# A depthwise convolution moved from VectorE to TensorE, in a two-block transformer kernel

## Chip, cores and metric

The kernel runs on one core of one Trainium2 chip. The metric is the device time of one execution in microseconds, the median of several runs. Below, PE is TensorE, PEld its loading of weights, DVE is VectorE, ACT ScalarE, POOL GpSimd; SP is the engine that only issues DMAs.

## What is computed

The reference has two blocks on 256 positions of 1024 channels. The first has two layers with modulation: the vectors `c` and `c_ctx` go through SiLU and a 1024 x 6144 matrix per layer, and give six rows (shift, scale and gate, twice). Layer 0 works on two streams, `x` and `ctx` (512 columns together), layer 1 on `x` alone (256 columns). A layer normalises, modulates, multiplies by `w_in`, and splits the product among four mixers: attention, a Fourier mixer, a convolution module and a pooling mixer. Their results are joined, multiplied by `w_out`, and a gated FFN follows. The second block has dilated attention, a spatial gating unit and another gated FFN, and is not touched by the change. The convolution module, cut to what matters:

```python
def conv_module(a, dw_w, dw_b, ln_g, ln_b, w_pw):
    glu = a[..., :W_CONV] * jax.nn.sigmoid(a[..., W_CONV:])
    y = lax.conv_general_dilated(glu, dw_w[:, None, :], window_strides=(1,), padding=[(15, 15)],
                                 feature_group_count=W_CONV) + dw_b     # 31 taps, each channel by itself
    y = jax.nn.silu(layer_norm(y, ln_g, ln_b))
    return y @ w_pw                                                     # W_CONV = 256
```

## The kernel before

Channels lie on the 128 partitions, positions along the columns; 256 channels are two halves, `f` = 0 and 1. The large products take f32 weights apart into a high part (cast on ACT, L244) and a low one (subtraction on DVE, L246) and do three passes (L274 to L276, or L299 to L301). Weights come in pieces of 512 KB on SP's queue, in the order of use, into four buffers `raw`.

**The start.** SP loads the first quarter of modulation weights for layer 0 (`mod_load`, four pieces), the input `XC` (four pieces), two pieces of `w_in`, the second quarter of the modulation (four) and the third group (four, two pieces of `w_in`, four). TensorE is ordered by hand here: `mod_mm` multiplies the weights with SiLU of `c` in column groups of 32 (tile `p_mod`, L464), `mod_cols` transposes the result into columns; `p_ss` (L531) sums squares over the partitions, `p_rb` (L538) spreads the inverse root, and `in0_k` makes the normalised input (n on ACT, L505 and L506, low part on DVE, L507) and starts the product `p_c` of the convolution's 512 input rows, which is the first main product. The other ten rows of modulation are not done by TensorE: `mod_bg` loads 512 KB per step into one of four buffers `wm` on ACT's queue, behind a one-element copy on POOL (L422) that holds the load back until an earlier operation is done, and DVE does two weighted sums per step (`jg`, L427, and `wm`, L429: called a pair below).

**The order.** Outside the start a planner writes the program: each chain of work is a generator that yields the time it thinks it needs; `spawn` starts one, `tick` moves the clock as TensorE's main products are emitted and lets due chains emit their next step, `join` waits for a chain. SP's queue is in the order of the code. Each engine then works its list in order.

**The convolution.** The gated unit (`sg` on ACT, then L688 on DVE) writes `GP`, with 15 columns of zeros on either side. `conv_diag` makes eight diagonal 128 x 128 matrices per half of the taps' weights (on POOL for layer 0, on ACT for layer 1); they lie in two of the four `wm` buffers. `conv_pe` does eight taps per half on TensorE (`p_cv`, L624), each a product of a diagonal matrix with `GP` shifted by a column; `conv_taps` does the other 23 on DVE, one operation each (L632, L636), and adds TensorE's part (L640). Then `conv_ln` takes the mean and the variance over channels on TensorE (`p_mean`, `p_var`), and normalises. `mod_bg` is spawned with the two tap chains as its conditions, so that in layer 0 the modulation's pairs start when the taps are done.

**After it** come attention (`p_qt` transposes queries and keys, `p_s` scores, `pe` exponentials on ACT with a minimum `ast` from DVE, L740, `pT` copies of the transposed ones, `p_o`), the Fourier mixer (`p_fa`, `p_fy`, `p_fw`), the pooling mixer (`UP`, POOL's sums, `p_pl`), and the output product `p_wo`.

Of the kernel before, what the change touches and what calls it, by code (L numbers as in the profile page):

```python
# [24 lines left out]
F32 = mybir.dt.float32  # L25
# [3 lines left out]
OP = mybir.AluOpType  # L29
AX = mybir.AxisListType  # L30

D = 1024
# [6 lines left out]
GW = T + 2 * PAD  # L39
# [6 lines left out]
NPE = 8  # L46
CVD, FOD = 0.9, 1
BG0, BG1 = 2.4, 2.0
SPL, SPH = {"wo1": 3}, (1,)
# [56 lines left out]
for _n, _w in (("c", 16), ("bmod0", 48), ("bmod1", 48), ("g1_0", 8), ("g1_1", 8), ("g2_0", 8),  # L106
               ("g2_1", 8), ("dw_0", 62), ("dw_1", 62), ("db_0", 2), ("db_1", 2), ("lg_0", 2), ("lg_1", 2),
               ("lb_0", 2), ("lb_1", 2), ("ps_0", 2), ("ps_1", 2), ("n1", 8), ("n2", 8), ("fg", 8), ("bs", 8)):
    PK[_n] = _o
    _o += _w  # L110
# [42 lines left out]
def tile_kernel(ctx, tc, xin, pk_d, rows_d, lc_d, bc_d, wmod0, wmod, win, wout, wfi, wfo, wsm, win2w, win2, wproj, wout2,  # L153
# [30 lines left out]
    V.memset(ones, 1.0)  # L184
    mhalf = cpool.tile([128, 12], F32, name="mhalf")
# [9 lines left out]
    G.tensor_scalar(P("dw_0", 0, 124), P("dw_0", 0, 124), 0.5, None, op0=OP.mult)  # L195
# [40 lines left out]
    def split_to(i):  # L236
        while ld["split"] < min(i, len(halves)):
# [7 lines left out]
            every = SPL.get(halves[j][2], 0) or (1 if j in SPH else 0)  # L245
# [224 lines left out]
    def mod_cols(g):  # L470
# [4 lines left out]
        pt = psm("p_modt")  # L475
# [38 lines left out]
    mod_load(0, 0, 4)  # L514
    for i in range(4):
        SP.dma_start(XC[:, 2 * i:2 * i + 2], xin[:, 2 * i:2 * i + 2])
    dma_to(2)
    mod_load(1, 0, 4)
    mod_load(2, 0, 4)
    dma_to(WB)  # L520
    mod_load(2, 4, 8)
    with tc.manual_schedule(engines={mybir.EngineType.PE}):
        mod_mm(0, 0, 4)
        mod_cols(0)
        new_ss(True)
# [3 lines left out]
        for i in range(4):  # L529
            for n, ss in enumerate(ss_t["ss"]):  # L530
                PE.matmul(p[:, i:i + 1], ss[:, 128 * i:128 * i + 128], ones, start=n == 0, stop=n == 1)  # L531
        r = rsqrt(p[:, :4], 4, 1.0 / D, True)
        ld["lim"] = WB
        split_to(2)
        mod_mm(1, 0, 2)
# [3 lines left out]
        mod_mm(1, 2, 4)  # L539
# [3 lines left out]
        split_to(WB)  # L543
        in0_k(2)
        mod_mm(2, 4, 8)
        in0_k(3, lambda: mod_cols(2))
        for k in range(4, KT):
            in0_k(k)
    ld["lim"] = 10 ** 6
    dma_to(WB + RAW)  # L550
    SP.dma_start(rows, bass.AP(tensor=rows_d.tensor, offset=rows_d.offset, ap=[[0, 128], [1, 512]]))
    SP.dma_start(lc, lc_d)

    SP.dma_start(scb.rearrange("p s n -> p (s n)"), bass.AP(tensor=rows_d.tensor, offset=rows_d.offset + 1536,
                                                            ap=[[0, 128], [1, 2048]]))
    for s in range(2):
        S.activation(scb[:, s], scb[:, s], AF.Silu)
# [5 lines left out]
    for l in range(2):  # L563
# [4 lines left out]
        with ExitStack() as mctx:  # L568
# [6 lines left out]
            UP = mp.tile([128, ns, UW], F32, name="UP")  # L575
            S2 = mp.tile([128, ns, UW], F32, name="S2")
            S4 = mp.tile([128, ns, UW], F32, name="S4")
            G.memset(UP[:, :, 0:POOL_PAD], 0.0)
            G.memset(UP[:, :, POOL_PAD + T:], 0.0)
            U = mp.tile([128, 2, N], F32, name="U")  # L580
# [4 lines left out]
            QT = [mp.tile([128, 2, 256], F32, name=f"QT{s}") for s in streams]  # L585

# [20 lines left out]
            cps = {}  # L607

            def conv_diag(f):

                w = lpool.tile([128, D], F32, tag="wm", name="cdg", bufs=WMB)
                for j in range(NPE):
                    tap = pk[:, PK[f"dw_{l}"] + f * TAPS + j:PK[f"dw_{l}"] + f * TAPS + j + 1]
                    if l == 0:
                        G.tensor_scalar(w[:, 128 * j:128 * j + 128], ident, tap, None, op0=OP.mult)
                    else:
                        S.activation(w[:, 128 * j:128 * j + 128], ident, AF.Copy, scale=tap)
                return w

            def conv_pe(f, w):  # L620

                cps[f] = psm("p_cv")
                for j in range(NPE):
                    PE.matmul(cps[f][:, :N].rearrange("p (s t) -> p s t", t=T), w[:, 128 * j:128 * j + 128],  # L624
                              GP[:, f, :, j:j + T], start=j == 0, stop=j == NPE - 1)
                    tick(0.0017 * N)

            def conv_taps(f, delay):
                y = Y[:, f].rearrange("p (s t) -> p s t", t=T)
                dw = PK[f"dw_{l}"] + f * TAPS  # L630
                per = 0.35 * ns
                V.tensor_scalar(y, GP[:, f, :, NPE:NPE + T], pk[:, dw + NPE:dw + NPE + 1], P(f"db_{l}", f), op0=OP.mult,  # L632
                                op1=OP.add)
                yield per + delay
                for j in range(NPE + 1, TAPS):
                    V.scalar_tensor_tensor(y, GP[:, f, :, j:j + T], pk[:, dw + j:dw + j + 1], y, op0=OP.mult, op1=OP.add)  # L636
                    yield per + delay
                while f not in cps:
                    yield 0.3
                V.tensor_tensor(Y[:, f], cps[f][:, :N], Y[:, f], op=OP.add)  # L640
                yield per
                G.tensor_copy(snap, Y[:, f, 0:1])
                pace[0] = snap
# [3 lines left out]
            def conv_ln(t0, t1):  # L647

                yield from wait(t0, t1)
# [86 lines left out]
            def att_unit(s, t, i, j, pT, sums, sp):  # L736
# [5 lines left out]
                pe = mp.tile([128, 512], F32, tag="pe", name="pe", bufs=PEB)  # L742
# [808 lines left out]
```

## Time and profile before

| | us |
|---|---|
| median of 3 runs (lowest, highest) | 1340.57 (1340.22, 1340.75) |
| the profiled execution | 1341.05 |
| its span in the trace | 1339.3 |
| TensorE busy | 1300.0 (97%) |
| DVE busy | 931.9 (70%) |
| ACT busy | 621.4 (46%) |
| POOL busy | 256.7 (19%) |

The time of a run is taken on the device around the program; the span is from the first to the last instruction in the trace of one more execution. The busy time of TensorE is that of its matmuls, whose loads of weights overlap with it. A share over the whole span says little about one stage; the rows further below are therefore taken by stretches of the span.

### The profile page before, as it was taken

The page shows a single profiled execution, that of the slowest core. Times are in us where ns is not written, and L with a number is a line of the kernel's source. Part 1 is how long each engine was busy: PE and PEld are TensorE (multiplying, and loading weights), DVE is VectorE, ACT ScalarE, POOL GpSimd, SP SyncE. Part 2 cuts the span into 40 slices and gives each one's busy share as a digit, 9 for nine tenths or more (in the row PEclk, how much of TensorE's full clock was granted, in tenths as well). Part 3 has the DMA queues.
Part 4 walks back from the last instruction along what each step waited for, and adds up shares of the span by engine and source line. Part 5 has one row for each costly group of instructions (what it writes and reads, how often), then busy time and mean ns, then how long its engine had stood idle before and what let it go on. Part 6 is the DMA issues. An engine that isn't in the chain of part 4 may idle for free.

```text
span 1339.3 us, 20667 instructions
## 1 busy us (share of the span) xinstructions
PE 1300.0 (97%) x7764; PEld 1107.6 (83%) x7764; DVE 931.9 (70%) x1658; ACT 621.4 (46%) x1045; POOL 256.7 (19%) x310
## 2 busy tenths in 40 slices
PE   5999989899999999999999999999999999999997
PEld 4786569788888888899789999888788889888886
DVE  3697997999883333359667666657675777888754
ACT  4434534322132222245565554445675655655542
POOL 4134543243310000133420000010110002211100
PEclk9999999999999999999999999999999999999999
DMA  9624453677883222334135554675344344555463
GB/s 370 221 79 149 134 173 99 244 250 245 300 299 119 95 86 65 102 130 145 45 106 191 178 187 152 189 259 185 129 147 157 135 160 171 191 190 186 154 190 102
DMA packets 66612, 224.67 MB, mean 168 GB/s; under 512 B 7504, under 2 KB 8656, under 8 KB 66384
## 3 DMA queue, kind: packets, MB, share of 16 engines
q1 hardware_dynamic: 53968, 179.21, 39.8%
q10 hardware_dynamic: 12080, 42.50, 9.5%
q0 software_dynamic: 464, 1.64, 0.3%
q8 instruction: 61, 1.00, 0.3%
q14 instruction: 39, 0.32, 0.1%
HBM read 222.27 MB, written 1.05 MB: 167 GB/s over the span
## 4 chain that ended last, share of the span: by engine, by line
PE 87%; DVE 5%; DMA 2%; ACT 2%; issue 2%; POOL 1%; POOLq 0%; SPq 0%; DVEq 0%; ACTq 0%
PE p_dn L283 6%; PE p_ua L275 5%; PE p_ua L276 5%; PE p_ua L274 4%; PE p_ug L276 4%; PE p_ug L275 4%; PE p_ug L274 4%; PE p_ga L283 3%; PE p_gg L283 3%; PE p_dn L274 3%; PE p_dn L275 3%; PE p_dn L284 3%; PE p_dn L276 3%; PE p_gt L283 2%; PE p_wo L276 2%; PE p_wo L275 2%
## 5 line engine op out<-in xcount | busy, mean ns | idle before, releaser
L246 DVE TENSOR_TENSOR wl<-raw,wh 128x1024 fp32r<-128x1024 f32 (+2 forms) x340 | 393.6, 1159 | 249.2 <-ACT wh L244 247.7
L244 ACT CAST wh<-raw 128x1024 fp32r<-128x1024 f32 (+1 forms) x344 | 333.8, 974 | 317.9 <-PE p_ug L275 86.6
L339 POOL TENSOR_TENSOR ss<-ss,sq 128x256 f32<-128x256 f32 (+1 forms) x43 | 45.3, 1054 | 441.5 <-ACT sq L338 295.1
L275 PE MATMUL p_ua<-A,wh 128*128 128x258 f32 (+2 forms) x368 | 122.3, 332 | 3.5 <-DVE A L365 3.5
L283 PE MATMUL p_dn<-H,wh 128*128 128x512 f32 x352 | 124.1, 397 | 0.0
L276 PE MATMUL p_ug<-A,wl 128*128 128x258 f32 (+2 forms) x368 | 122.3, 332 | 0.0
L276 PE MATMUL p_ua<-A,wl 128*128 128x258 f32 (+2 forms) x368 | 122.1, 332 | 0.0
L275 PE MATMUL p_ug<-A,wh 128*128 128x258 f32 (+2 forms) x368 | 121.9, 331 | 0.0
L274 PE MATMUL p_ua<-A,wh 128*128 128x258 f32 (+2 forms) x368 | 121.6, 331 | 0.0
L274 PE MATMUL p_ug<-A,wh 128*128 128x258 f32 (+2 forms) x368 | 121.6, 331 | 0.0
L429 DVE SCALAR_TENSOR_TENSOR wm<-wm,scb 128x1024 f32<-128x1024 f32 x80 | 98.2, 1232 | 10.8 <-DMA wm<-in_wmod 10.7
L284 PE MATMUL p_dn<-H,wl 128*128 128x256 f32 x352 | 98.5, 281 | 0.0
L283 PEld LDWEIGHTS p_dn<-H,wh 128*128 128x128 f32 x352 | 66.0, 188 | 16.1
L275 PEld LDWEIGHTS p_ua<-A,wh 128*128 128x128 f32 x368 | 69.4, 189 | 11.0 <-DVE A L365 3.9
L275 PEld LDWEIGHTS p_ug<-A,wh 128*128 128x128 f32 x368 | 69.5, 189 | 7.2
L276 PEld LDWEIGHTS p_ua<-A,wl 128*128 128x128 f32 x368 | 69.5, 189 | 6.9
L274 PEld LDWEIGHTS p_ug<-A,wh 128*128 128x128 f32 x368 | 69.3, 188 | 7.0
L274 PEld LDWEIGHTS p_ua<-A,wh 128*128 128x128 f32 x368 | 69.3, 188 | 7.0
L276 PEld LDWEIGHTS p_ug<-A,wl 128*128 128x128 f32 x368 | 69.4, 189 | 6.9
L274 PE MATMUL p_dn<-H,wh 128*128 128x512 f32 (+1 forms) x198 | 72.4, 367 | 0.0
L275 PE MATMUL p_dn<-H,wh 128*128 128x512 f32 (+1 forms) x198 | 72.4, 366 | 0.0
L276 PE MATMUL p_dn<-H,wl 128*128 128x512 f32 (+1 forms) x198 | 72.4, 366 | 0.0
(380 smaller groups left out, 3130.4 us busy)
## 6 DMA issues: line engine op xcount, KB each, us to landing
raw<-in_wfi SPq DMA_DIRECT2D x88, 512.0 KB, 3.8
wm<-in_wmod ACTq DMA_DIRECT2D x80, 512.0 KB, 4.5
raw<-in_win SPq DMA_DIRECT2D x44, 512.0 KB, 3.8
raw<-in_wgu SPq DMA_DIRECT2D x44, 512.0 KB, 3.7
raw<-in_win2w SPq DMA_DIRECT2D x40, 512.0 KB, 4.0
raw<-in_wout SPq DMA_DIRECT2D x24, 512.0 KB, 3.7
raw<-in_wfo SPq DMA_DIRECT2D x32, 384.0 KB, 3.1
raw<-in_wfo SPq DMA_DIRECT2D x32, 320.0 KB, 3.2
```

The costliest lines, as they stand in the source:

```text
L244: S.copy(h[:, :n], raw[:, :n])
L246: (G if every and j % every == 0 else V).tensor_tensor(lo[:, :n], raw[:, :n], h[:, :n].bitcast(F32), op=OP.subtract)
L274: PE.matmul(ps, w[0], a[:, 0], start=first, stop=False, **kw)
L275: PE.matmul(ps, w[0], a[:, 1], start=False, stop=False, **kw)
L276: ins = PE.matmul(ps, w[1], a[:, 0], start=False, stop=last, **kw)
L283: PE.matmul(p.rearrange("p (h n) -> p h n", h=2), w[0], a, start=first, stop=False)
L284: PE.matmul(p[:, 0:256], w[1], a[:, 0], start=False, stop=last)
L339: (eng or G).tensor_tensor(ss[0][:, cs], ss[0][:, cs], sq[:, :n], op=OP.add)
L429: V.scalar_tensor_tensor(w, w, 1.0, scb[:, 0], op0=OP.mult, op1=OP.mult, accum_out=modv[:, l, part, 0, k:k + 1])
```

## The change

**The convolution.** DVE's taps and the diagonal matrices go. `conv_shift` copies the gated rows within the chip's memory: for each half, for each group `g` of 32 channels and each shift `j` of 0 to 3, one DMA on SP's queue takes 32 partitions of `GP` from column `j` on and puts them on partitions 32 j to 32 j + 31 of `GS`; 32 copies per layer. A matmul on such a group then contracts 32 channels times four taps: its weights are 128 x 32, four small diagonal matrices under each other, its output is 32 partitions wide. `conv` does eight steps (of 4 taps, 32 in all, the last one zero) for four groups, 64 matmuls per layer, and ACT adds the bias as it takes the sum (L633). The weights of a half are made by one POOL operation. `conv` is spawned with a delay of 8.0 of the planner's time, and joined before attention starts; the pool that holds `GS` is closed then, and the tiles of the pooling mixer and of attention (`UP`, `S2`, `S4`, `U`, `pe`, `pT`) are opened in its place.

**The modulation.** `mod_bg` has no condition any more; its pacing copy reads the gated rows until the convolution is done.

**The start.** SP loads the input first, then two pieces of modulation weights, one of `w_in`, two, one, the four of the second quarter, all eight of the third group, and then `w_in`. TensorE sums the squares first, in one sum per column instead of two; the modulation products follow. Transposed rows go to the second half of the modulation's own PSUM tile. The low part of the second piece of `w_in` is made by DVE, not POOL. `rows`, `lc`, `scb` are loaded, and the normalised input released for the later products, a little earlier. The SiLU of `scb` (SiLU of `c`'s rows) is written behind the gated unit.

```diff
-NPE = 8
-CVD, FOD = 0.9, 1
+CVS = 8.0
+FOD = 1
...
+    id32 = cpool.tile([128, 32], F32, name="id32")
+    V.tensor_reduce(id32, ident.rearrange("p (g c) -> p c g", c=32), axis=AX.X, op=OP.add)
...
-    mod_load(0, 0, 4)
     for i in range(4):
         SP.dma_start(XC[:, 2 * i:2 * i + 2], xin[:, 2 * i:2 * i + 2])
+    mod_load(0, 0, 2)
+    dma_to(1)
+    mod_load(0, 2, 4)
     dma_to(2)
     mod_load(1, 0, 4)
-    mod_load(2, 0, 4)
+    mod_load(2, 0, 8)
     dma_to(WB)
-    mod_load(2, 4, 8)
...
-        mod_mm(0, 0, 4)
-        mod_cols(0)
-        new_ss(True)
+        new_ss(False)
...
-        split_to(2)
-        mod_mm(1, 0, 2)
+        split_to(1)
+        mod_mm(0, 0, 3)
         rb = psm("p_rb")
...
-        mod_mm(1, 2, 4)
+        mod_mm(0, 3, 4)
+        mod_cols(0)
+        mod_mm(1, 0, 4)
         in0_k(0, lambda: mod_cols(1))
...
             def conv_diag(f):
...
+                w = lpool.tile([128, D], F32, tag="wm", name="cdg", bufs=WMB).rearrange("p (q c) -> p q c", c=32)
+                G.tensor_tensor(w, id32[:, None, :].to_broadcast([128, 32, 32]),
+                                P(f"dw_{l}", 32 * f, 32)[:, :, None].to_broadcast([128, 32, 32]), op=OP.mult)
                 return w
...
+            def conv_shift(f):
+
+                gs = gp.tile([128, 4, ns, SW], F32, tag="GS", name="GS", bufs=2)
+                for g in range(4):
+                    for j in range(4):
+                        SP.dma_start(gs[32 * j:32 * j + 32, g], GP[32 * g:32 * g + 32, f, :, j:j + SW])
+                return gs
+
+            def conv(gss):
+
+                for f in range(2):
+                    p = psm("p_cv")
+                    for j in range(8):
+                        for g in range(4):
+                            PE.matmul(p[32 * g:32 * g + 32, :N].rearrange("p (s t) -> p s t", t=T), cdg[f][:, 4 * j + g],
+                                      gss[f][:, g, :, 4 * j:4 * j + T], start=j == 0, stop=j == 7)
+                        yield 0.35 * ns
+                    yield 0.4
+                    S.activation(Y[:, f], p[:, :N], AF.Identity, bias=P(f"db_{l}", f))
+                    yield 0.6
+                G.tensor_copy(snap, Y[:, 1, 0:1])
                 pace[0] = snap
...
-            cv0 = spawn(conv_taps(0, CVD))
-            cv1 = spawn(conv_taps(1, CVD), 0.5)
-            cv = spawn(conv_ln(cv0, cv1))
+            cvm = spawn(conv([conv_shift(f) for f in range(2)]), CVS)
+            cv = spawn(conv_ln(cvm))
             if l == 0:
+                pace[0] = GP[:, 1, 0, PAD:PAD + 1]
                 spawn(mod_bg([(0, 2, True, BG0), (0, 4, True, BG0), (0, 3, True, BG0), (0, 5, True, BG1),
                               (1, 1, True, BG1), (1, 0, True, BG1), (1, 2, False, BG1), (1, 4, False, BG1),
-                              (1, 3, False, BG1), (1, 5, False, BG1)], cv0, cv1))
+                              (1, 3, False, BG1), (1, 5, False, BG1)]))
...
-            for f in range(2):
-                conv_pe(f, cdg[f])
+
+            join(cvm)
+            gctx.close()
+            ap = mctx.enter_context(tc.tile_pool(name=f"a{l}", bufs=1))
```

The order of instructions shows what the lines make of it. First TensorE's list at the start, before:

```order
L464 MATMUL p_mod<-rawm,scf 32x128 x32
L477 MATMUL p_modt<-ident,row 128x128
L531 MATMUL p_ss<-ones,ss 128x1
L531 MATMUL p_ss<-ones,ssl 128x1
L531 MATMUL p_ss<-ones,ss 128x1
L531 MATMUL p_ss<-ones,ssl 128x1
L531 MATMUL p_ss<-ones,ss 128x1
L531 MATMUL p_ss<-ones,ssl 128x1
L531 MATMUL p_ss<-ones,ss 128x1
L531 MATMUL p_ss<-ones,ssl 128x1
L464 MATMUL p_mod<-rawm,scf 32x128 x16
L538 MATMUL p_rb<-ident,rs_r 128x128 x4
L464 MATMUL p_mod<-rawm,scf 32x128 x16
L274 MATMUL p_c<-A_73,wh 128x512
```
and after:

```order
L532 MATMUL p_ss<-ones,ss 128x1 x4
L467 MATMUL p_mod<-rawm,scf 32x128 x24
L539 MATMUL p_rb<-ident,rs_r 128x128 x4
L467 MATMUL p_mod<-rawm,scf 32x128 x8
L480 MATMUL p_mod<-ident,row 128x128
L467 MATMUL p_mod<-rawm,scf 32x128 x32
L277 MATMUL p_c<-A_73,wh 128x512
```
The sum of squares has moved from behind the first quarter of the modulation to the front, and all of the second quarter now stands behind the spreading of the root (`p_rb`).

Next TensorE's list in layer 0, where the convolution's passes stand. Before, behind the products `p_q`, `p_kv` and `p_f`, between transposes of queries and keys, 16 matmuls in blocks of 1, 7 and 8:

```order
L727 MATMUL p_qt<-ident,qt_809 128x128 x3
L624 MATMUL p_cv<-GP,cdg 128x512
L727 MATMUL p_qt<-ident,qt_843 128x128 x3
L624 MATMUL p_cv<-GP,cdg 128x512 x7
L275 MATMUL p_f<-A_73,wh 128x512
```
After, among the products of keys and values, from the third pass of `p_kv` on; here the first lone matmul:

```order
L302 MATMUL p_kv<-wh,A_73 128x256
L303 MATMUL p_kv<-wl,A_73 128x256
L304 MATMUL p_kv<-wh,A_73 128x256
L629 MATMUL p_cv<-GS,cdg 32x512
L302 MATMUL p_kv<-wh,A_73 128x256
```
Further down in the same list stands the first long run, with two of the lone ones behind it:

```order
L302 MATMUL p_kv<-wh,A_73 128x256
L629 MATMUL p_cv<-GS,cdg 32x512 x29
L303 MATMUL p_kv<-wl,A_73 128x256
L304 MATMUL p_kv<-wh,A_73 128x256
L302 MATMUL p_kv<-wh,A_73 128x256
L303 MATMUL p_kv<-wl,A_73 128x256
L304 MATMUL p_kv<-wh,A_73 128x256
L629 MATMUL p_cv<-GS,cdg 32x512
L302 MATMUL p_kv<-wh,A_73 128x256
L303 MATMUL p_kv<-wl,A_73 128x256
L629 MATMUL p_cv<-GS,cdg 32x512
L304 MATMUL p_kv<-wh,A_73 128x256
```
In layer 0 there are six lone matmuls and two runs of 29, the second one within `p_f`; in layer 1 five lone ones and runs of 30 and 29.

Last, DVE's list in layer 0 from the gated unit on. Before:

```order
L246 TENSOR_TENSOR wl<-raw,wh 128x1024 x3
L688 SCALAR_TENSOR_TENSOR GP<-sg,p_c 128x2x256
L246 TENSOR_TENSOR wl<-raw,wh 128x1024
L632 TENSOR_SCALAR Y<-GP,pk 128x512
L688 SCALAR_TENSOR_TENSOR GP<-sg,p_c 128x2x256
L636 SCALAR_TENSOR_TENSOR Y<-GP,pk,Y 128x512
L632 TENSOR_SCALAR Y<-GP,pk 128x512
L636 SCALAR_TENSOR_TENSOR Y<-GP,pk,Y 128x512 x10
L246 TENSOR_TENSOR wl<-raw,wh 128x1024
```
After:

```order
L249 TENSOR_TENSOR wl<-raw,wh 128x1024
L681 SCALAR_TENSOR_TENSOR GP<-sg,p_c 128x2x256
L249 TENSOR_TENSOR wl<-raw,wh 128x1024
L681 SCALAR_TENSOR_TENSOR GP<-sg,p_c 128x2x256
L430 SCALAR_TENSOR_TENSOR jg,modv<-wm,scb 128x1024
L432 SCALAR_TENSOR_TENSOR wm,modv<-wm,scb 128x1024
L430 SCALAR_TENSOR_TENSOR jg,modv<-wm,scb 128x1024
L432 SCALAR_TENSOR_TENSOR wm,modv<-wm,scb 128x1024
L249 TENSOR_TENSOR wl<-raw,wh 128x1024 x2
L430 SCALAR_TENSOR_TENSOR jg,modv<-wm,scb 128x1024
```
and, behind the end of the convolution:

```order
L715 TENSOR_TENSOR qt_1047<-qt_1047,rs_r 128x384
L430 SCALAR_TENSOR_TENSOR jg,modv<-wm,scb 128x1024
L432 SCALAR_TENSOR_TENSOR wm,modv<-wm,scb 128x1024
L430 SCALAR_TENSOR_TENSOR jg,modv<-wm,scb 128x1024
L649 TENSOR_TENSOR Y<-Y,p_mean 128x512 x2
L432 SCALAR_TENSOR_TENSOR wm,modv<-wm,scb 128x1024
L430 SCALAR_TENSOR_TENSOR jg,modv<-wm,scb 128x1024
L249 TENSOR_TENSOR wl<-raw,wh 128x1024 x2
L432 SCALAR_TENSOR_TENSOR wm,modv<-wm,scb 128x1024
L430 SCALAR_TENSOR_TENSOR jg,modv<-wm,scb 128x1024
L733 TENSOR_REDUCE ast<-p_s 128x1 x2
L325 TENSOR_SCALAR rs_v<-p_var 128x4
```
The pairs (`jg`, `wm`) follow the gated unit directly, and stand ahead of the operations that take away the mean (L649) and start the inverse root of the variance (L325).

## Rows read from the trace of the kernel before

**Rows 1.** the page, busy time, share of the span, instructions of each engine
```profile
PE 1300.0 (97%) x7764; PEld 1107.6 (83%) x7764; DVE 931.9 (70%) x1658; ACT 621.4 (46%) x1045; POOL 256.7 (19%) x310
```

**Rows 2.** busy time by stretch (columns in the first line)
```profile
core 0: us, PE busy (x) PEld busy (x) DVE busy (x) ACT busy (x) POOL busy (x), PEclk, DMA share, GB/s
...
56.60:195.30 138.70, 132.02 (x705) 94.44 (x705) 128.45 (x232) 57.81 (x136) 59.80 (x59) 0.99 0.43 139
...
27.10:30.50 3.40, 3.40 (x11) 2.52 (x10) 1.80 (x8) 1.43 (x3) 0.00 (x0) 0.50 1.03 412
143.10:146.60 3.50, 3.50 (x12) 1.89 (x12) 3.50 (x4) 2.25 (x5) 3.35 (x3) 0.51 0.24 96
```

**Rows 3.** timeline of TensorE, first 26 us (start, duration, operation, records, idle before)
```profile
5.42 1.08 PE L464 MATMUL p_mod<-rawm,scf 128*32 128x128 f32 x16 [5.42 <-DMA rawm<-in_wmod]
...
9.45 1.08 PE L464 MATMUL p_mod<-rawm,scf 128*32 128x128 f32 x16 [0.17 <-DMA rawm<-in_wmod]
...
16.74 0.59 PE L531 MATMUL p_ss<-ones,ss 128*128 128x1 f32 x2 [5.29 <-DVE ss L339]
...
25.91 0.49 PE L274 MATMUL p_c<-A,wh 128*128 128x512 f32 x1 [1.38 <-ACT A L506]
```

**Rows 4.** the same view, one modulation product between main products
```profile
33.32 0.39 PE L275 MATMUL p_c<-A,wh 128*128 128x512 f32 x1
33.55 0.39 PE L276 MATMUL p_c<-A,wl 128*128 128x512 f32 x1
33.87 1.93 PE L464 MATMUL p_mod<-rawm,scf 128*32 128x256 f32 x32
...
36.08 0.39 PE L275 MATMUL p_c<-A,wh 128*128 128x512 f32 x1
```

**Rows 5.** the same view, the convolution's passes in either layer
```profile
105.87 7.04 PE L624 MATMUL p_cv<-GP,cdg 128*128 128x512 f32 x16
...
633.07 6.21 PE L624 MATMUL p_cv<-GP,cdg 128*128 128x256 f32 x28
```

**Rows 6.** waits of TensorE, 56.6 to 195.5 us (total, times, longest)
```profile
PE p_s L747 <- ACT pe L743: 1.9, 1, 1.9
PE p_wo L274 <- ACT A L795: 1.1, 1, 1.1
PE p_wo L274 <- DVE XC L948: 1.0, 1, 1.0
PE p_wo L275 <- DVE A L796: 1.0, 1, 1.0
PE p_s L763 <- ACT pT L749: 0.9, 1, 0.9
```

**Rows 7.** groups of DVE instructions, 56.6 to 195.3 us
```profile
L636 DVE SCALAR_TENSOR_TENSOR Y<-GP,pk,Y 128x512 f32<-128x512 f32 x44 | 31.4, 753 | 0.0
L427 DVE SCALAR_TENSOR_TENSOR jg<-wm,scb 128x1024 f32<-128x1024 f32 x22 | 28.8, 1307 | 0.5 <-DMA wm<-in_wmod 0.5
```

**Rows 8.** instructions on the modulation's buffer, 100 to 215 us, and who waited
```profile
L427 DVE SCALAR_TENSOR_TENSOR jg<-wm,scb x24: 1214/1219/2277, 117.6 to 205.2; 128x1024 f32<-128x1024 f32 x24
...
  ACT pT L749: 2.3, 2
...
DMA to landing us min/median/max: 3.3/3.6/5.7
```

**Rows 9.** waits of TensorE, 593 to 705 us
```profile
PE p_s L763 <- DVE Y L640: 1.2, 1, 1.2
PE p_wo L274 <- ACT A L795: 1.0, 1, 1.0
```

**Rows 10.** issues of DMAs (durations in ns), and one small load (us to landing)
```profile
L450 SPq DMA_DIRECT2D rawm<-in_wmod x16: 327/328/432, 1.2 to 26.2; - x16
...
pk<-in_pk SPq DMA_DIRECT2D x1, 8.0 KB, 2.0
```

**Rows 11.** timeline of the SP queue, 600 to 625 us
```profile
603.26 7.94 SPq L232 DMA_DIRECT2D raw<-in_win  x4
```

More of the change, by code (lines that the diff above doesn't have):

```diff
@@ L529, in tile_kernel @@
         for i in range(4):
-            for n, ss in enumerate(ss_t["ss"]):
-                PE.matmul(p[:, i:i + 1], ss[:, 128 * i:128 * i + 128], ones, start=n == 0, stop=n == 1)
+            PE.matmul(p[:, i:i + 1], ss_t["ss"][0][:, 128 * i:128 * i + 128], ones, start=True, stop=True)
         r = rsqrt(p[:, :4], 4, 1.0 / D, True)
         ld["lim"] = WB
-        split_to(2)
-        mod_mm(1, 0, 2)
+        split_to(1)
+        mod_mm(0, 0, 3)
         rb = psm("p_rb")
@@ L542, in tile_kernel @@
         mod_mm(2, 0, 4)
-        split_to(WB)
         in0_k(2)
         mod_mm(2, 4, 8)
+        split_to(WB)
+        ld["lim"] = 10 ** 6
+        dma_to(WB + RAW)
+        SP.dma_start(rows, bass.AP(tensor=rows_d.tensor, offset=rows_d.offset, ap=[[0, 128], [1, 512]]))
+        SP.dma_start(lc, lc_d)
+        SP.dma_start(scb.rearrange("p s n -> p (s n)"), bass.AP(tensor=rows_d.tensor, offset=rows_d.offset + 1536,
+                                                                ap=[[0, 128], [1, 2048]]))
         in0_k(3, lambda: mod_cols(2))
@@ L548, in tile_kernel @@
             in0_k(k)
[L549 to L557, printed above, removed]
+            if k == 5:
+                with tc.issue_after(ahs[-1].ins), tc.issue_after(als[-1].ins):
+                    done(n_, 0, 0)
+                    done(n_, 1, 0)
     sctx.close()
@@ L606, in tile_kernel @@
             acc = {}
-            cps = {}
             def conv_diag(f):
[L611 to L617, printed above, removed]
-                return w
@@ L620, in conv_pe @@
[L620 to L642, printed above, removed]
+                w = lpool.tile([128, D], F32, tag="wm", name="cdg", bufs=WMB).rearrange("p (q c) -> p q c", c=32)
@@ L643, in conv_taps, with conv_ln @@
                 pace[0] = snap
             in_done = []
-            def conv_ln(t0, t1):
-                yield from wait(t0, t1)
+            def conv_ln(t0):
+                yield from wait(t0)
                 mean = psm("p_mean")
@@ L766, in attention @@
                         for j in range(2):
[L767 removed]
+                            pT = ap.tile([128, 512], F32, tag="PT", name="pT", bufs=PTB)
                             pts.append(pT)
@@ L877, in tile_kernel @@
                 glu(1, ps4[2], ps4[3])
+                for s in range(2):
+                    S.activation(scb[:, s], scb[:, s], AF.Silu)
                 with tc.issue_after(ahs[-1].ins), tc.issue_after(als[-1].ins):
@@ L915, in tile_kernel @@
             done(n_, 3)
-            for f in range(2):
-                conv_pe(f, cdg[f])
+            join(cvm)
+            gctx.close()
+            ap = mctx.enter_context(tc.tile_pool(name=f"a{l}", bufs=1))
+            UP = ap.tile([128, ns, UW], F32, name="UP")
+            S2 = ap.tile([128, ns, UW], F32, name="S2")
+            S4 = ap.tile([128, ns, UW], F32, name="S4")
+            G.memset(UP[:, :, 0:POOL_PAD], 0.0)
+            G.memset(UP[:, :, POOL_PAD + T:], 0.0)
+            U = ap.tile([128, 2, N], F32, name="U")
             at = []
```

32 lines of the change are left out of this document (15 added, 17 removed).

## The prediction, made before the changed kernel was run

> **What bounds the kernel now.** I began with the busy times. TensorE works 1300.0 us of the 1339.3 us span [rows 1]: a reader should see that whatever the change takes off another engine can pay only inside the 39 us in which TensorE is idle, and that whatever it adds to TensorE lies on the path in full. So I split the span into stages and looked for TensorE's idle time in the two that the change touches, and for stretches at the lower clock. From the first layer's query product to its output product (56.6 to 195.3 us) TensorE is busy 132.02 of 138.70 us; and two stretches, of 3.4 and 3.5 us, run at a granted clock of 0.50 and 0.51, the 1.2 GHz level, where every pass takes twice as long: each costs about 1.7 us [rows 2]. Before 25.91 us there is the start, which waits for data.
>
> All sums below are made against the profiled execution, 1341.05 us; the median of the three runs is 1340.57, 0.48 lower. I apply the differences to the median.
>
> **The start.** Pieces of 512 KB come one after another; the first rows of the modulation product start at 5.42 and 9.45 us for pieces 1 and 4, so a piece takes (9.45 - 5.42)/3 = 1.34 us. The sum of squares waits 5.29 us for DVE, which waits for the input, pieces 5 to 8, and the first product of the main stream starts at 25.91 us, after a chain of normalisation [rows 3]. Afterwards the input comes first, so that this chain ends some 5 us earlier. But the first main product also needs the second quarter of the modulation weights, behind which it stands in TensorE's order; its last piece is the 14th in either order of the queue (before 4 of modulation, 4 of input, 2 of weights, 4 of modulation; after 4 of input, 2 of modulation, 1 of weights, 2, 1 and 4). The 14th lands at about 5.4 + 13 x 1.34 = 22.8 us; one piece's passes and the change of matmul kind add 0.7. I take 23.5 instead of 25.9: **-2.4 us**. From below the gain is 0 if the half-clock stretch right behind it grows by as much, from above 4.1, if that stretch goes too (2.4 + 1.7). From there to 56.6 us the later weights have room: the order of the queue only swaps pieces that are used 5 us and more after they land.
>
> **The convolution on TensorE.** Before, sixteen 128-wide matmuls per layer: a run of 16 records takes 7.04 us in the first layer, so a record is (7.04 - 0.59)/15 = 0.43 us, and in the second (6.21 - 0.38)/27 = 0.216 us [rows 5]. A matmul on f32 is two records; 32 records make 13.8 and 6.9 us. Afterwards there are 64 matmuls, 32 outputs wide, in four column groups. What four groups cost is read from the modulation products, which have this form: 32 records of 256 columns take 1.93 us, that is eight steps of (1.93 - 0.38)/7 = 0.22, four records to a step [rows 4]. So a round of four matmuls costs what one costs. But the order tells that not all come four together: in the first layer six stand alone between other products and two runs have 29 (8 rounds), 22 rounds of 0.86 = 18.9 us, **+5.1**. In the second three stand alone, then runs of 30 and 29 with two lone ones between them, 21 rounds of 0.43 = 9.0 us, **+2.1**.
>
> **The changes of matmul kind.** Between two products of the usual kind an excursion to the 32-wide kind costs more than its rounds: from the pass at 33.55 to that at 36.08 us are 2.53 us; less two usual passes (0.23 each) and eight steps (1.76) leaves 0.3 [rows 4]. The order has 8 such excursions in the first layer and 7 in the second: 15 x 0.28 = 4.2, less some 0.4 for the excursions that the old convolution made: **+3.8**. The rows bound it between 0 (the excursion's ends hide behind loads of weights, as in a long run) and 4.5. The Trainium skill, "TensorEngine Tiling (Array Packing)", section Key Properties, says that changing the tiling mode drains the engine, which speaks against lone 32-wide matmuls; it gives no figure. By that rule every excursion costs, and the row agrees; without a price for it the sum would be 3.8 us lower.
>
> **The waits that go in the first layer.** DVE loses 44 taps, 31.4 us [rows 7], and starts at once on the modulation pairs, two operations of 1.3 us each; 24 pairs whose first operations lay between 117.6 and 205.2 us [rows 8] lie, by the order, between 62 and some 165 us. So the tail of the stage is free of them. The waits there [rows 6]: 1.9 us for the first exponential (behind the convolution's end and a table load; afterwards 18 passes lie over it), 0.9 for a copy that stood on ACT behind the issue of a modulation load (ACT waited 2.3 us in all on POOL's release of those buffers [rows 8]), 1.0 and 1.0 for DVE operations that stood behind a pair, and half of the 1.1 on ACT's cast, which follows a DVE product. With the half-clock stretch at 143.1 us, which comes right behind the second of them, that is 1.9 + 0.9 + 1.0 + 1.0 + 0.5 + 1.7 = **-7.0**. What is late next is a copy of the exponentials and the rest of the cast, 1.3 us, which stay.
>
> **New waits.** Where the convolution used to stand, the pairs now share two buffers, since the weights of the convolution hold the other two until it ends. A load takes 3.3 to 5.7 us from issue [rows 8], so two pairs take about 2.5 + 5 us and ten are done at the convolution's end, 47 us behind the last main product; then the operation that takes the mean away stands behind a pair whose load was released only then. I expect 0.5 us where up to 6 are possible, since the row of DVE waiting for such a load has 0.5 [rows 7]: **+0.5**.
>
> **The copies.** Thirty-two small DMAs per layer wait for the gated unit (first layer: two DVE operations that start at 57.3 and 59.5 us). At 0.33 us an issue, and 2.0 to land as the nearest, small load took [rows 10], four copies of one group are there 3.4 us behind the unit and all sixteen of one half after 7.3; the first matmul stands behind 99 passes of 256 columns, each half of 0.23, at 56.6 + 11.7 = 68 us, the second layer's, behind 80 from 606.6 us, at 616. There the copies stand in the queue behind the last four loads of input weights, issued by 603.26 + 7.94 = 611.2 us [rows 11]: group 0 lands at 614.6. **0**, bounded by 0 and 3 us a layer.
>
> **The second layer.** The wait of 1.2 us for DVE's last tap goes; of that for ACT's cast, 1.0, I take half [rows 9]: **-1.7**. Making the weights costs two POOL operations in place of sixteen in the first layer, with 60 us of cover, and of eight on ACT per half in the second, where ACT is not waited for; without that cover the first lone matmul would be late by as much as they take. The single sum of squares in place of two costs TensorE four matmuls less while it waits anyway.
>
> Sum: -2.4 + 5.1 + 2.1 + 3.8 - 7.0 + 0.5 - 1.7 = +0.4, and 1340.57 + 0.4 = **1341.0 us**. A difference below 0.2%, 2.7 us, can't be told from no change here.
>
> **The rivals.**
> 1. *TensorE never waits.* With DVE lighter in both layers the new waits don't come (-0.5), the 1.3 us that I left go, so does the start's half-clock stretch (-1.7), and the second layer gives 1.0 more; the lone matmuls then cost a little less than the excursion row says (-1). Together -5.5: 1335.5. For it: TensorE waited for nothing between 56.6 and 114 us with DVE nearly full. Against it: the stretches at half clock have come after quite different histories, and some of those waits are on ACT.
> 2. *The modulation in the way of the attention* (slower). Pairs stand in DVE's order ahead of the mean, the variance and the exponentials' minima; their buffers are released by POOL, whose order has the clearing of the pool mixer's tile in front, which waits for the convolution's last matmul; and ACT issues the loads in order between its copies. The price: one load's landing, 4.5 us, less the 13 passes of 0.23 that lie over it, 3.0, at the variance; one more pair, 2.5, at its inverse root; and ACT's 2.3 once more: 6.3 in place of 0.5, which gives 1346.8. It decides as soon as new waits pass 2.8 us. For it: the order, and ACT's waits before. Against it: the passes of two products lie in between.
> 3. *The copies come late.* If a copy holds the queue for 0.8 us, the second layer's first sixteen are there at 611.2 + 12.8 + 2 = 626 and all at 639 us, where TensorE comes to the two long runs at some 625 and 635: +4, 1345. No row shows copies within the chip's own memory; the loads' issues speak against it.
> 4. *The column groups don't run side by side:* 64 x 0.86 + 64 x 0.43 = 82.6 in place of 18.9 + 9.0 = 27.9 us: +55, 1396. The modulation rows speak against it. A fifth, that a part of the change does nothing, holds for one edit: the SiLU of c's rows stands in ACT's order ahead of the gated unit in either kernel. It is worth nothing in the sum.
>
> **How the numbers follow.** My forecast has 0.47 (its terms may each be off by 1 to 2 us: 0.05 of it falls below 1337.9, 0.35 within, 0.07 above 1343.3), rival 1 0.28, rival 2 0.17 (0.03 of it within), rival 3 0.06 (0.01 within), rival 4 0.02. Faster: 0.05 + 0.28 = 0.33. Same: 0.35 + 0.03 + 0.01 = 0.39. Slower: 0.28. The range reaches into rivals 1 and 2, from 1334.0 to 1347.0; rival 4 and the far ends of the bounds are left out.
>
> **What would show it.** Right: the first main product at 23 to 24 us; records of the convolution in fours, the next four 0.43 us later, 18 to 20 us of them in the first layer; no wait of TensorE for DVE or ACT at the output product; the same stage, from the last main product to the first row of the output's second half, 138 to 141 us long. Wrong: a TensorE wait of over 2 us for a copy of the gated rows, for the variance or its root, or for an exponential; records of the convolution one after another; a first main product at 26 us.

## The result and the profile after

The changed kernel takes **1351.63 us** (median of 4 runs, 1350.09 to 1353.75) against 1340.66 of the kernel before in the same session: a ratio of 1.0083, 95% interval 1.0070 to 1.0096. It is slower by some 11 us, 4.6 above the top of the predicted range. The profiled execution took 1351.17 us (span 1349.5), 10.1 above that of before. The page's first part:

```profile
PE 1307.9 (97%) x7948; PEld 1102.8 (82%) x7948; DVE 889.2 (66%) x1565; ACT 618.2 (46%) x1033; POOL 232.8 (17%) x295
```

Against [rows 1], DVE is 42.7 us lighter, as the change meant, and TensorE 7.9 us busier. The span after, in stretches bounded by TensorE's products, and one stretch inside (columns as in [rows 2]):

```profile
23.40:53.30 29.90, 27.83 (x168) 19.84 (x163) 14.87 (x29) 19.13 (x32) 2.47 (x10) 1.00 0.92 350
53.30:224.80 171.50, 163.52 (x1002) 117.63 (x1003) 119.57 (x218) 67.49 (x154) 60.13 (x72) 1.00 0.44 136
...
600.20:615.80 15.60, 14.53 (x104) 14.06 (x104) 12.55 (x26) 7.72 (x15) 3.06 (x5) 0.89 0.52 166
615.80:897.10 281.30, 279.60 (x2157) 256.98 (x2158) 181.61 (x327) 151.09 (x253) 37.72 (x45) 1.00 0.49 157
...
602.10:605.40 3.30, 3.30 (x16) 3.30 (x17) 2.93 (x9) 1.56 (x4) 1.16 (x3) 0.50 0.76 245
```

Layer 0's mixers before, in the same columns:

```profile
56.60:219.50 162.90, 156.21 (x908) 118.54 (x908) 149.09 (x266) 67.26 (x153) 72.76 (x71) 0.99 0.40 131
```

The same stretches of both kernels, in us:

| stretch | before | after | |
|---|---|---|---|
| to the first main product | 25.9 | 23.4 | -2.5 |
| to layer 0's first query product | 30.7 | 29.9 | -0.8 |
| layer 0's mixers, to the first FFN product | 162.9 | 171.5 | **+8.6** |
| layer 0's FFN | 374.2 | 375.4 | +1.2 |
| layer 1, to its first query product | 12.9 | 15.6 | **+2.7** |
| rest of layer 1 | 281.4 | 281.3 | -0.1 |
| second block | 451.3 | 452.4 | +1.1 |

So most of the loss is in layer 0's mixers. There, before, TensorE was busy 156.21 us, of which 1.7 were lost to the half clock (half of the stretch at 143.1 us, [rows 2]), and idle 6.7: 154.5 of its own work and 8.4 of loss. After it is busy 163.5 at the full clock and idle 8.0. **Own work rose by 9.0, and the losses fell by only 0.4.** Both can be followed in the trace.

The own work, in the timeline of TensorE behind the gated unit (columns as in [rows 3]):

```profile
66.55 1.02 PE L629 MATMUL p_cv<-GS,cdg 128*32 128x512 f32 x2 [1.32 <-DMA GS<-GP]
...
68.42 0.28 PE L303 MATMUL p_kv<-wl,A 128*128 128x256 f32 x1
68.63 1.05 PE L629 MATMUL p_cv<-GS,cdg 128*32 128x512 f32 x2
69.61 0.39 PE L304 MATMUL p_kv<-wh,A 128*128 128x256 f32 x1
69.83 0.28 PE L302 MATMUL p_kv<-wh,A 128*128 128x256 f32 x1
...
76.52 7.05 PE L629 MATMUL p_cv<-GS,cdg 128*32 128x512 f32 x58
```

A lone matmul (two records) makes the passes at 68.42 and 69.83 stand 1.41 us apart, where two passes take 0.24 (they start 0.12 apart): 1.17 us. A run of 58 records takes 7.05 us, as long as the sixteen 128-wide records of [rows 5]: the column groups do run four at a time. So a lone matmul pays 1.17 us for a quarter of what a full round of four does in 0.86.

The losses, as waits of TensorE from 50 to 225 us (total, times, longest):

```profile
PE p_pl L856 <- POOL S L851: 2.4, 2, 1.2
PE p_fw L831 <- DVE U L824: 1.7, 1, 1.7
PE p_cv L629 <- DMA GS<-GP: 1.3, 1, 1.3
PE p_wo L277 <- ACT A L788: 1.0, 1, 1.0
PE p_q L302 <- ACT sg L680: 0.9, 1, 0.9
PE p_o L776 <- ACT pT L742: 0.9, 2, 0.5
PE p_s L756 <- DVE awo L785: 0.6, 1, 0.6
```

(`S` are the pooling mixer's sums, `U` the Fourier mixer's, `awo` the attention's result, `fce` a copy in the Fourier mixer, `QK` copies of queries and keys.) Of [rows 6] only the first `p_wo` row is left. The first three rows are new, 5.4 us, at places where TensorE did not wait before; the last stands at the score product that waited 0.9 us for a copy before, and now 0.6 for DVE. Together these four are 6.0 us. (`p_q`'s wait lies ahead of 53.3.) Two more views show what came ahead of them. First, what ACT waited for, 53 to 200 us (total, times, longest), where [rows 8] has 2.3 for one row:

```profile
ACT awo L784 <- POOL wm L425: 6.5, 2, 4.0
...
ACT fce L821 <- POOL wm L425: 4.2, 2, 2.5
...
ACT QK L898 <- POOL wm L425: 2.1, 1, 2.1
...
ACT wh L247 <- POOL wm L425: 2.0, 1, 2.0
```

With two smaller ones ACT stood 17.9 us behind POOL's release of the modulation's buffers; before, with two loads of an activation table that [rows 8] leaves out (1.6), it was 3.9. Second, POOL's timeline ahead of `p_pl` (columns as for TensorE): the modulation's closing sums (`modv`) and releases (`wm`) stand between the pooling mixer's own sums (`S`).

```profile
133.29 1.18 POOL L440 TENSOR_TENSOR modv<-modv,pk 128x8 f32<-128x8 f32 x1
134.45 0.22 POOL L439 TENSOR_SCALAR modv<-modv 128x8 f32<-128x8 f32 x1
134.75 1.28 POOL L849 TENSOR_TENSOR S<-S,lc 64x512 f32<-64x512 f32 x1
136.12 1.07 POOL L440 TENSOR_TENSOR modv<-modv,pk 128x8 f32<-128x8 f32 x1
137.13 1.18 POOL L425 COPY wm<-snap 128x1 f32<-128x1 f32 x1
138.27 1.26 POOL L851 TENSOR_TENSOR S<-S,UP 128x512 f32<-128x512 f32 x1
```

Ahead of `p_fw` it is DVE: its timeline has the two operations of the pairs from 147.16 to 151.11 us, then the last `U` at 151.31, and TensorE, after its wait of 1.7 us, goes on at 151.64.

### The profile page after: what moved, and what is told of

It is laid out like the page before. It is cut to its first block, busy times and chain, and to the rows that moved or that the text cites. A ratio compares the mean times of both kernels' runs of the same rounds, so it can differ in the third digit from the quotient of the medians.

```text
span 1349.5 us, 21017 instructions
## 1 busy us (share of the span) xinstructions
PE 1307.9 (97%) x7948; PEld 1102.8 (82%) x7948; DVE 889.2 (66%) x1565; ACT 618.2 (46%) x1033; POOL 232.8 (17%) x295
## 4 chain that ended last, share of the span: by engine, by line
PE 86%; DMA 5%; DVE 4%; POOL 2%; issue 2%; ACT 1%; SPq 0%; DVEq 0%; POOLq 0%; ACTq 0%
PE p_dn L286 6%; PE p_ua L278 5%; PE p_ua L279 5%; PE p_ua L277 5%; PE p_ug L279 5%; PE p_ug L278 5%; PE p_ug L277 5%; PE p_ga L286 3%; PE p_gg L286 3%; PE p_dn L287 3%; PE p_gt L286 2%; PE p_cv L629 2%; DMA wm<-in_wmod 2%; PE p_dn L279 2%; PE p_dn L277 2%
## 5 line engine op out<-in xcount | busy, mean ns | idle before, releaser
L432 DVE SCALAR_TENSOR_TENSOR wm<-wm,scb 128x1024 f32<-128x1024 f32 x80 | 101.0, 1267 | 11.9 <-DMA wm<-in_wmod 11.3
L286 PEld LDWEIGHTS p_dn<-H,wh 128*128 128x128 f32 x352 | 65.9, 188 | 15.6
```

Source lines behind the costliest of these rows:

```text
L286: PE.matmul(p.rearrange("p (h n) -> p h n", h=2), w[0], a, start=first, stop=False)
L432: V.scalar_tensor_tensor(w, w, 1.0, scb[:, 0], op0=OP.mult, op1=OP.mult, accum_out=modv[:, l, part, 0, k:k + 1])
```

## The experiments

Theory A: the loss is TensorE's own work, above all the lone 32-wide matmuls. Theory B: it is the waits that the early modulation pairs make on ACT, POOL and DVE. A third possibility is the start. Each run's ratio is against the kernel before in its own session, whose medians were 1340.67 to 1341.35.

**1. The start alone**, in the kernel before (all else of the change left out).

```diff
-    mod_load(0, 0, 4)
     for i in range(4):
         SP.dma_start(XC[:, 2 * i:2 * i + 2], xin[:, 2 * i:2 * i + 2])
+    mod_load(0, 0, 2)
...
```

> The kernel before, with the new start alone (input first, one sum of squares, modulation products behind it); the convolution stays as before. In the changed kernel the last main product of the start ends 3.3 us earlier than before, 2.5 from the earlier first product and the rest from the half-clock stretch that is gone. If the start pays by itself: 1340.6 - 3.3 = 1337.3 (1336.5 to 1338.5). Rival, DVE's taps are the longer chain of the next stage and take the gain back at their end: 1339.5 to 1341.

1340.22 us, ratio 0.9993 (0.9983 to 1.0003). Busy time by stretch in layer 0's mixers:

```profile
54.50:219.20 164.70, 157.74 (x906) 118.79 (x907) 149.32 (x266) 67.05 (x152) 72.78 (x71) 0.98 0.42 128
115.80:119.20 3.40, 3.40 (x10) 1.42 (x10) 3.05 (x7) 1.08 (x5) 0.18 (x1) 0.50 0.93 325
143.10:146.50 3.40, 3.19 (x10) 1.31 (x6) 3.40 (x5) 1.79 (x4) 3.25 (x3) 0.50 0.22 89
```

The time can't be told from no change, as the rival said, but for another reason. The stage begins 2.1 us earlier (54.5 for 56.6), and 1.8 of it is lost in the stage: it has a second stretch at the 1.2 GHz level, at 115.8, shortly behind the 1.9 us wait for the first exponential, which this kernel still has. Its waits are those of the kernel before to 0.3 us in sum, so DVE's taps did not take the gain back.

**2. The convolution without the start** (the changed kernel with the old start).

> The changed kernel with the old start: what the convolution's and the modulation's move cost without the start. In the changed kernel the start ends 3.3 us earlier than before; alone it gave the kernel before no more than about 1 us. If the two add: 1351.6 + 3.3 = 1354.9 (1354 to 1356.5). If the start's gain is lost in the next stage here too: 1351 to 1353.

1354.37 us, ratio 1.0107 (1.0090 to 1.0123), 2.7 us above the changed kernel. So the new start is worth 2.7 us in the changed kernel, and the convolution and its pairs cost 13.7. In the profiles 1.7 of the gain stands at layer 0's first query product (55.0 and 53.3 us); the rest of it lies in the mixers, where the kernel with the old start waits 2.1 us at `p_pl` in one piece and has a half-clock stretch of 3.4 us behind it.

**3. The matmuls of the convolution kept together**, 32 of each half in one run, groups in turn.

```diff
-                    for j in range(8):
-                        for g in range(4):
...
-                        yield 0.35 * ns
-                    yield 0.4
+                    with tc.manual_schedule(engines={mybir.EngineType.PE}):
+                        for j in range(8):
+                            for g in (3, 0, 1, 2):
...
+                    yield 2.8 * ns + 0.4
```

> The changed kernel, with the 32 matmuls of each half of the convolution together: they are kept in one order, and each round begins with the group whose copies are issued last, so that none goes ahead alone. Theory A, the extra time is TensorE's own work: rounds fall from 22 to 16 of 0.86 us and from 21 to 16 of 0.43 (5.2 + 2.2), excursions to the narrow kind from 15 to 4 of 0.28 (3.1): 1351.6 - 10.4 = 1341.2 (1340 to 1343). If lone matmuls cost only their round: 1344.3. Theory B, the extra time is waits behind the modulation pairs and the copies on DVE, POOL and ACT, which this leaves as they are: 1349 to 1352.

**4. The pairs started behind the convolution again**, with the lone matmuls, and **5. both edits**.

```diff
-                              (1, 3, False, BG1), (1, 5, False, BG1)]))
+                              (1, 3, False, BG1), (1, 5, False, BG1)], cvm))
```

> The changed kernel, with the modulation pairs started only when the convolution is done, as the kernel before had it. Theory B: the waits for the pool mixer (1.2 + 1.2), the Fourier product (1.7), the copies of the gated rows (1.3) and the exponentials' copies (1.1) go, the three at the output product (1.0 each) come back partly: 1346 to 1348. Theory A: 1350 to 1352, since TensorE's work stays.

> Both edits. Theory A alone: as with packing alone, 1341. Theory B alone: as with the late pairs alone, 1347. If both hold and add: 1336 to 1338, below the kernel before.

With the matmuls together: 1348.13 us (1.0053, 1.0034 to 1.0071). Late pairs: 1348.62 (1.0062, 1.0047 to 1.0077). Both: 1339.95 (0.9996, 0.9985 to 1.0007). Either edit alone lies outside what either theory gave it; the two together miss the 1336 to 1338 of their sum, yet undo the whole loss. Here is the layer-0 stage of the late pairs, alone first, then with the matmuls together, and the two runs of the latter in TensorE's timeline:

```profile
54.80:224.10 169.30, 163.83 (x1002) 117.23 (x1003) 118.91 (x218) 68.23 (x154) 64.22 (x72) 0.99 0.46 138
```

```profile
52.90:216.70 163.80, 158.38 (x1003) 119.20 (x1004) 117.00 (x218) 67.92 (x154) 65.26 (x72) 0.99 0.47 143
```

```profile
70.52 7.07 PE L630 MATMUL p_cv<-GS,cdg 128*32 128x512 f32 x64
...
80.97 7.49 PE L630 MATMUL p_cv<-GS,cdg 128*32 128x512 f32 x64
```

With the matmuls together TensorE is busy 5.5 us less for the same passes, and by the medians the kernel is 8.7 us faster (1348.62 - 1339.95). The two profiled executions are 10.0 apart: 5.5 lie in this stage, 1.7 in layer 1's mixers and 0.9 ahead of them, and 1.7 ahead of the first main product (24.6 and 22.9 us), which the edit doesn't touch. TensorE's own work is 5.5 us less here and 2.6 less in layer 1's mixers (90.6 and 88.0): theory A holds, with about 8 us. It does not cover all of the own work: less the 1.7 of a half-clock stretch, 156.7 us are left in layer 0's mixers, 2.2 above the kernel before, and what makes these was not tested. Packing alone, with early pairs, brought only 3.5. Its stage, two stretches inside, and its longest waits:

```profile
53.60:226.10 172.50, 164.93 (x1003) 128.68 (x1004) 120.02 (x218) 67.83 (x155) 67.05 (x72) 0.95 0.44 135
136.10:149.70 13.60, 12.51 (x36) 7.21 (x37) 13.60 (x24) 8.16 (x18) 12.20 (x10) 0.50 0.42 135
197.50:200.90 3.40, 3.33 (x8) 2.68 (x9) 0.65 (x2) 0.02 (x1) 0.00 (x0) 0.50 0.00 0
```

```profile
PE p_s L756 <- ACT pT L742: 3.1, 2, 2.6
PE p_cv L630 <- DMA GS<-GP: 2.8, 2, 2.6
```

The own work did fall: 164.93 less 7.9 (half of the busy time in the two stretches at 0.50) is 157.0, 6.5 below the changed kernel's 163.5. But around the end of a wait of 2.6 us for `pT`, at 136.67, begin 13.6 us at the lower level, and they took 6.3 back. This execution, 1350.43 us, is the slowest of the run's four, so the others may have lost less. In the kernel with both edits a wait of 2.8 us at the same line is followed by 3.4 us at 0.50. Begun with the group that is copied last, the convolution here also waits 2.6 us for its copies; in run 5 it waits for none.

Late pairs alone bring 3.0 us by the medians; the two intervals overlap a little (1.0047 to 1.0077, and 1.0070 to 1.0096), so the size is uncertain. The waits at `p_pl`, `p_fw` and for `awo` are gone, which shows that the pairs' place made them; others came instead, again 5.5 us idle in all, and 1.7 at half clock:

```profile
PE p_fa L803 <- ACT fa L808: 3.2, 1, 3.2
PE p_q L302 <- ACT sg L680: 1.4, 1, 1.4
PE p_o L776 <- ACT pT L742: 1.1, 2, 0.7
...
```

**6. The modulation's loads issued by POOL instead of ACT**, in the changed kernel, and **7.** with both edits of 5. If ACT's standing behind POOL's release were the cause, this takes it away.

```diff
-                S.dma_start(w, wmod[l, 8 * part + k])
+                G.dma_start(w, wmod[l, 8 * part + k])
```

> The changed kernel, with the modulation's loads issued on POOL's queue instead of ACT's. ACT then never stands behind the release of a buffer (in the changed kernel it does so for 15.8 us in all between 100 and 200 us). Theory B in this form, ACT's order is what makes TensorE wait in the first layer: of the 8.0 us of idle time from the first query product to the FFN, some 3 go (the waits for ACT's copies and for what follows them): 1348 to 1349. Rival, the waits come from DVE's and POOL's own lists (pool mixer 2.4, Fourier 1.7): no change, 1350 to 1352, or slower, since POOL has more to issue: 1352 to 1355.

> Packed convolution and late pairs, with the modulation's loads issued on POOL's queue. With the loads on ACT's queue one wait of 2.8 us for ACT's copy of the exponentials, which stood behind such an issue for 3.1 us, and the half-clock stretch right behind it (1.7) remain. If ACT's order is the cause: 1340.0 - 4.5 = 1335.5 (1334.5 to 1337). If POOL, busy with the pool mixer, is late with the loads all the same and DVE's pairs move back into the output product: 1339 to 1341.

1362.71 us (1.0161, 1.0147 to 1.0175), and 1342.42 (1.0014, 1.0005 to 1.0023): worse than the changed kernel by 11.1, more than either range allowed, and than 5 by 2.5. In the first TensorE is idle 14.0 us in the stage, at a mean clock of 0.95. Its longest waits:

```profile
PE p_lnr L661 <- POOL rs_r L326: 4.3, 1, 4.3
PE p_s L740 <- ACT pe L736: 3.4, 3, 2.5
PE p_fa L803 <- ACT pe L736: 2.2, 1, 2.2
```

Now it is POOL's list that holds the inverse root of the variance. The theory that ACT alone was at fault falls.

**8. The release on DVE instead of POOL**, in the changed kernel, and **9.** with both edits of 5.

```diff
-                G.tensor_copy(w[:, 0:1], pace[0])
+                V.tensor_copy(w[:, 0:1], pace[0])
```

> The changed kernel, with the one-element pacing copies into the modulation's buffers made by DVE, which is also the engine that frees those buffers, in place of POOL. With the loads on POOL's queue the changed kernel became 11 us slower, so where the loads stand decides, but POOL's list was then in the way itself. If POOL's late release (its list has the pool mixer, the rope products and the modulation's closing sums) is what ACT and then TensorE wait for: the pool mixer's 2.4 us and the waits behind ACT go, 1346 to 1348. If DVE's own list is the cause (pairs ahead of the attention's operations): 1350 to 1353.

> Packed convolution and late pairs, loads on ACT's queue again, pacing copies on DVE. There one wait of 2.8 us remained (ACT stood 3.1 us behind a load whose release POOL gave late, between two sums of the pool mixer), with a half-clock stretch behind it. If POOL's place in the release is the cause: 1340.0 - 4.5 = 1335.5 (1334.5 to 1337), below the kernel before. If ACT waits as long for DVE's release: 1339 to 1341.

1355.63 us (1.0116, 1.0098 to 1.0133), and 1341.12 (1.0004, 0.9995 to 1.0012). With early pairs it is worse than the changed kernel and than either range:

```profile
PE p_pl L856 <- POOL S L851: 3.2, 1, 3.2
PE p_fw L831 <- DVE U L824: 2.9, 1, 2.9
PE p_s L756 <- DVE awo L785: 2.2, 1, 2.2
```

The pooling mixer's sums are late with the release off POOL as well. With both edits of 5 the 2.8 us wait for `pT` shrinks to 0.5, and `p_q` and `awo` waits of 1.3 and 1.2 take its place. That it was POOL's release alone falls too.

**10 to 12. SiLU of `c`'s rows really behind the gated unit** (with 5 and loads on POOL; with 5 and the release on DVE; with 5 alone). "The run before" in the first two texts is 7 and 9.

```diff
-                glu(1, ps4[2], ps4[3])
-                for s in range(2):
-                    S.activation(scb[:, s], scb[:, s], AF.Silu)
+                sg1 = glu(1, ps4[2], ps4[3])
+                with tc.issue_after(sg1.ins):
+                    for s in range(2):
+                        S.activation(scb[:, s], scb[:, s], AF.Silu)
```

> As the run before, and the SiLU of c's rows really behind the gated unit on ACT, where its source line stands. The first query product waits 0.7 us for the gated unit's activation, which stands behind that SiLU (2.0 us) and its load. If that is why: 0.7 less than the run before, 1334.8. If the wait has another cause (the cast of weights in front of it): no difference.

> As the run before, with the SiLU of c's rows behind the gated unit on ACT. The first query product's wait of 0.7 us was gone in the one kernel that had this edit, whose time did not differ from its neighbour's. 0.7 less than the run before: 1334.8; no difference if another operation fills the gap.

> Packed convolution and late pairs, pacing copies on POOL and loads on ACT as in the changed kernel, and the SiLU of c's rows behind the gated unit on ACT. If the 0.7 us wait of the first query product is worth its length: 1340.0 - 0.7 = 1339.3, and 1.3 below the kernel before, which is inside what a measurement can tell from no change. If waits only move: 1340 to 1341. A version clearly faster than the kernel before would need 1338 or less.

1342.37 us (1.0010, 1.0001 to 1.0019), 1339.52 (1.0000, 0.9990 to 1.0009) and 1339.16 (0.9987, 0.9975 to 0.9998). In the changed kernel ACT's timeline has the SiLU first, late because its load is:

```profile
49.83 2.01 ACT L872 ACTIVATE scb<-scb 128x1024 f32<-128x1024 f32 x2 [2.50 <-DMA scb<-in_rows]
52.68 0.59 ACT L680 ACTIVATE sg<-p_c 128x512 f32<-128x512 f32 x1
```

In the last kernel `sg` stands at 51.79, the SiLU at 53.70, and the wait at `p_q` is gone. It is the best version, 2.2 us below the kernel before. Its whole interval is below 1, but 0.13% is small beside the spread of the kernel before in that session, 1338.57 to 1344.84 us, and I don't call it faster. Its stage is still 164.3 us, with 5.9 idle.

## Why the prediction was wrong

| step | predicted | in the traces |
|---|---|---|
| start | -2.4 | -2.5, and -0.8 to the first query product |
| layer 0, TensorE's own work | +7.1 (5.1, and 8 of the 15 changes) | +9.0 |
| layer 0, waits that go, with the clock | -7.0 | -6.4 |
| layer 0, new waits for engines | +0.5 | +4.7 |
| layer 0, the copies | 0 | +1.3 |
| layer 1 (2.1 + 1.8 - 1.7) | +2.2 | +2.6 |
| layer 0's FFN, second block | 0 | +2.3 |
| sum | +0.4 | +10.2 |

**The step that failed** is the term of the new waits: "I expect 0.5 us where up to 6 are possible". They came to 4.7 us (2.4 at the pooling mixer, 1.7 at the Fourier mixer, 0.6 at the scores), and the copies, a term of their own at 0, to 1.3. The waits that go did go, nearly as priced: all of [rows 6] but the first `p_wo` row, 4.8 us, and 1.7 of half clock, 6.5 of the 7.0 (a wait that stayed grew by 0.2). So the losses only changed places. I had priced one new wait, by one row of DVE, at one place (the mean), where none came. What came was made by POOL's list (the pooling mixer) and DVE's list (the Fourier mixer and the scores); run 4, in which these waits are gone, shows that the pairs' place made them. Rival 2 was the right kind, pairs in the way, with a size (6.3) not far off, but at the wrong place; I gave it 0.17 since "the passes of two products lie in between". The passes did cover the mean and the variance, and did not cover what comes later. The rest of the miss is 1.9 of own work in layer 0, 0.4 in layer 1 and 2.3 in layer 0's FFN and the second block, less 0.9 that the start gave beyond its price.

**The price of the 32-wide kind was right.** An excursion cost 1.17 - 0.86 = 0.31 us where I took 0.28. Own work came out 1.9 higher: by the starts in the timeline the convolution takes 6.4 more than before and the product `p_kv` around it 1.5, 7.9 against 7.1; the other 1.1 is spread over products that I did not follow. The Trainium skill, "TensorEngine Tiling (Array Packing)", section Key Properties, has changes of tiling mode drain the engine. The trace agrees in so far as an excursion costs 0.31 us out and back; the drain itself it doesn't show.

**The start was right** where it was priced, 23.4 against 23.5 us, and the half-clock stretch behind it [rows 2] went too. Run 1 shows what I did not price: a gain at the start can be lost to the clock later (1.8 us in the one execution profiled).

**The copies** were not free. In layer 0 TensorE waited 1.3 us for them, within my bound of 3. An issue took 0.59 us at the median, not 0.33. A landing took 4.5 us at the median in layer 0, and the 2.0 that I took only in layer 1 (1.9). Over both:

```profile
L620 SPq DMA_DIRECT2D GS<-GP x64: 508/589/1222, 56.2 to 639.2; - x64
...
DMA to landing us min/median/max: 1.8/3.0/8.2
```

Rival 3 (0.8 us an issue) overstated it; in layer 1 no wait for a copy showed.

**The second layer** came out close in sum by luck, though its mixers came as priced. From its first query product on, and in its FFN alone, before and after:

```profile
606.60:888.00 281.40, 277.42 (x2062) 259.52 (x2061) 199.58 (x374) 149.97 (x249) 40.82 (x44) 1.00 0.48 154
696.80:888.00 191.20, 190.86 (x1416) 182.50 (x1415) 130.86 (x237) 99.98 (x140) 7.54 (x9) 1.00 0.57 184
707.80:897.10 189.30, 189.02 (x1417) 181.19 (x1416) 130.38 (x237) 99.93 (x140) 7.55 (x9) 1.00 0.58 185
```

In the mixers, which are the difference, TensorE's own work rose from 86.6 to 90.6 us, 4.0 where 3.9 was priced, and its idle time fell by 2.2 where 1.7 was. Two things that I did not price nearly cancel: ahead of them +2.7 (1.7 for the half-clock stretch at 602.1, 0.8 for the wait of `p_q` for `sg`), and -1.9 in the FFN, where the same passes take 1% less, for a reason that no run here shows. **Rivals 1 and 4 fall:** in layer 0 TensorE waits no less than before, and the groups run side by side. The fifth holds: the SiLU edit left ACT's order as it was.

**Open:** the 1.1 us of own work that I did not follow; the 2.3 us in layer 0's FFN (0.8 of it a wait for a low part of weights) and the second block; what sets which products become late each time; and whether some place for the pairs leaves fewer waits than the 4 to 6 us idle that the better versions share in layer 0's mixers, since none was found.

## What to carry to other kernels

A matmul form that pays by running several column groups side by side has to be kept together in TensorE's list; a planner that lets one of them slip between other products makes it cost more than all four together (1.17 us against 0.86 here, about 8 us of TensorE's work in two layers). Taking work off an engine that is not the bound frees no time by itself: what then moves up, here modulation pairs, meets other work in three engines' lists, and its price has to be looked for at every later wait of TensorE, not at the first. When a stage's waits seem to go, ask for the sum of idle and lost clock, not for the list: moving the issue or the release of the loads to another engine changed the list each time and never made the kernel faster.

## What the runs showed of the hardware

The granted clock of TensorE fell to 0.50, the 1.2 GHz level, around or shortly behind the end of waits of 1.9 to 3.2 us in runs 1 to 5, for some 3.4 us, in run 3 for 13.6. With what followed, the wait of 2.6 us for `pT` there cost 8.9. In the changed kernel, whose waits in layer 0's mixers were 1.7 us at the longest, no such stretch lay there. It is no rule: in the kernel before, the wait of 1.9 had none behind it, and the stretch at 143.1 us lay behind one of 0.9 [rows 2, 6]; in run 3 the wait of 2.6 us for the copies, which ended at 75.7 us, was followed by the full clock (1.00 to 84 us). The waits were not varied by themselves, so the link is read from the order in the traces, not shown by an experiment.

Small copies within the chip's memory landed 2.0 to 8.2 us after issue in layer 0 (71 KB each), and 1.8 to 4.6 us in layer 1 (35.5 KB), with medians of 4.5 and 1.9; size and the 512 KB loads beside them were not told apart. The Trainium skill, "DMA: Bandwidth & Descriptors", section "🔬 Anatomy of one DMA — SWDGE (gpsimd) path", puts a fixed cost of about 2 us on a DMA of GpSimd's queue. The copies here are on SP's queue: the quickest and layer 1's median are near that figure, layer 0's median is not.
